# Prompt attention: all matmuls of a unit in one fixed order on TensorE

## The chip, the cores and the metric

One core of one Trainium2 chip runs the kernel as a single program on five engines: TensorE (PE), VectorE (DVE), ScalarE (ACT), GpSimd (POOL) and SyncE (SP, which mostly issues transfers). Each engine runs its own instructions in the order in which they stand in its program and waits on the others by semaphores. The metric is the device time of one launch in microseconds (us); lower is better.

## What is computed

One layer of a hybrid decoder, for a prompt of 2048 tokens and a small decode batch. The change touches the prompt attention: 8 heads of 64, three dilated window patterns, and a merge of the three outputs by their softmax denominators. Cut to that:

```python
PATTERNS = ((128, 1), (512, 4), (2048, 16))
def dilated_prompt(q, k, v, window, dil):      # blocks of n = window // dil = 128 queries
    ...
    s = jnp.einsum('brhcie,brhcje->brhcij', qb, kk) * (E ** -0.5)   # keys: block before and own block
    ...
    s = jnp.where(mask, s, NEG)
    lse = jax.nn.logsumexp(s, axis=-1)
    p = jnp.exp(s - lse[..., None])
    o = jnp.einsum('brhcij,brhcje->brhcie', p, vv)
    ...
def combine_patterns(results):
    outs = jnp.stack([o for o, _ in results], axis=0)
    lses = jnp.stack([l for _, l in results], axis=0)
    w = jax.nn.softmax(lses, axis=0)
    return jnp.sum(w[..., None] * outs, axis=0)
```

After the attention come the output projection `w_o`, norms and a gated feed-forward network.

## The kernel before

**Stages.** The trace shows dense projections and sweeps up to about 780 us, the prompt attention from there to about 1140 us, and then the output projection and the feed-forward network, in which TensorE is nearly always busy, to the end. The change touches the middle stage alone.

**Units.** Heads are taken in four pairs `pr` 0 to 3. A pair goes through three patterns (`pat` 0 to 2) of four groups `g`. A group has two units in patterns 0 and 1, and one in pattern 2: 20 units per pair, 80 in all. They are numbered u0 to u79 here, so pair 0 ends with u19, pair 1 with u39, pair 2 with u59. `qk_` of a unit makes, for each of two heads, the scores in a PSUM tile `pas` (8 matmuls of up to 256 columns per unit in patterns 0 and 1, 16 of 128 in pattern 2; three buffers), the row minima of the masked, negated scores on DVE (into `ass`, six buffers) and the exponentials on ACT, in place. `t` turns these with 8 transposes per unit into `pat` (PSUM) and copies them to `apt` on ACT or DVE. `pv` multiplies by the values into `pao` (8 matmuls, each of which the trace shows as two records); at a group's end DVE copies `pao` to the output tile `aop` of the pattern.

**Shared buffers.** Outputs of the patterns rotate through five `aop` buffers, so that the copy for pattern 2 of pair 2 waits until the merge of pair 1 has last read pattern 1 of pair 1 (line 1215), pattern 0 of pair 2 until the merge of pair 0 has last read its output (line 1217), and pattern 0 of pair 3 until the merge of pair 1 has. In patterns 1 and 2 the queries come from gathered copies `aqg` that POOL makes (line 1118, two per group, five buffers, emitted two groups ahead): a gather waits until the scores of 2.5 groups earlier are done.

**The merge.** When a pair is done, `at_merge` runs beside the next pair's units: eight small matmuls (lines 1127, 1130), small steps on DVE and POOL (lines 1136 to 1166), weights written to memory (line 1184, POOL's queue) and read back broadcast (line 1173, POOL's queue), then on POOL twelve multiplies (line 1211), four adds (line 1215), four adds into `amo` (line 1217) and four stores (line 1219). `amo` has one buffer, which the merge's first steps share: each line 1217 waits until the store before it has landed, and a merge can't begin before the last store of the merge before has landed. They are called M0 to M3 here. M3 differs: it makes its weights on POOL and ACT (lines 1206, 1204), spreads them on TensorE (line 1208), multiplies on DVE (line 1209), and its last two adds into `amo` are on DVE (line 1217). The output projection's first part reads back what M3 stored.

**What sets the order.** The units are emitted in a software pipeline: `skew=(2, 2)` means that the transposes of the unit two back are emitted behind a unit's scores, followed by the values of that unit. The emitted order binds no engine: a scheduler works out, before the run, a fixed order for each engine from an estimate of when operands come, and tile buffers and data dependences are its only limits. So on TensorE scores, transposes and values of several units are mixed.

## Time and profile before

| | us |
|---|---|
| three runs | 2859.22, 2867.0, 2854.1 |
| median | 2859.22 |
| profiled execution, its own time | 2860.6 |
| span of its trace | 2858.6 |
| granted TensorE clock, mean | 0.978 of full |

The profiled execution's time is 2.0 us longer than the span of the trace, and 1.4 us above the median of the three runs. Over the whole span TensorE is busy 2726.4 us (95%), DVE 1854.4 (65%), ACT 1279.2 (45%) and POOL 598.6 (21%). These shares say little of the attention, which is about an eighth of the span: it must be read stretch by stretch. Line numbers below and in the text are those of the kernel before.

### The profile page before, as it was taken

The numbers are of one execution on the slowest core, as the hardware profiler recorded it, in microseconds if no ns is written. First come the engines' busy times: TensorE is split into PE (matmuls) and PEld (weight loads), VectorE is DVE, ScalarE is ACT, GpSimd is POOL, SyncE is SP. The second block draws the span as 40 slices with busy tenths as digits, with TensorE's granted clock in tenths as the row PEclk, the third lists the DMA queues.
The fourth block names the chain that finished last, engine by engine and source line by source line (L and its number), as shares of the span: only waits on it lengthen the run. The fifth ranks groups of instructions, "written<-read, shape, count | busy, mean of one in ns | idle before, by whom it ended". The sixth has DMA issues, their size and how long they took to land. (4 is left out here: it accounts for less than half of the span.)

```text
span 2858.6 us, 58660 instructions
## 1 busy us (share of the span) xinstructions
PE 2726.4 (95%) x22255; PEld 2545.2 (89%) x22255; DVE 1854.4 (65%) x4557; ACT 1279.2 (45%) x2958; POOL 598.6 (21%) x751
## 2 busy tenths in 40 slices
PE   7999999999998988899899999999999999999997
PEld 6788899787877766899799999999999999999997
DVE  7657654443355656456899888776667766666666
ACT  6535433332266765344565544443344433443332
POOL 3424242443324466112210003000020000200001
PEclk9999999999999998999899999999999999999998
DMA  8755445898888655347588758787587875876654
GB/s 296 252 179 188 163 147 168 309 335 321 281 176 177 145 128 111 99 154 268 188 309 300 248 208 308 276 294 266 194 321 282 294 261 192 325 256 218 217 193 146
DMA packets 285657, 657.09 MB, mean 230 GB/s; under 512 B 31856, under 2 KB 82672, under 8 KB 283328
## 3 DMA queue, kind: packets, MB, share of 16 engines
q1 hardware_dynamic: 254880, 576.50, 59.9%
q0 software_dynamic: 13408, 44.99, 5.2%
q10 hardware_dynamic: 17088, 31.86, 3.0%
q8 instruction: 175, 2.87, 0.4%
q14 instruction: 106, 0.87, 0.1%
HBM read 509.29 MB, written 143.94 MB: 229 GB/s over the span
## 5 line engine op out<-in xcount | busy, mean ns | idle before, releaser
L68 ACT ACTIVATE ws<-wr 128x512 fp32r<-128x512 f32 (+1 forms) x482 | 293.4, 616 | 437.0 <-PE pfe L1559 132.5
L90 PE MATMUL pfd<-hh,ws 128*128 128x264 f32 x2816 | 476.2, 285 | 9.2 <-ACT ws L68 5.4
L90 PEld LDWEIGHTS pfd<-hh,ws 128*128 128x128 f32 x2816 | 400.3, 189 | 12.6 <-ACT ws L68 7.0
L71 DVE TENSOR_TENSOR ws<-wr,ws 128x512 fp32r<-128x512 f32 (+1 forms) x482 | 319.7, 669 | 137.4 <-ACT ws L68 134.5
L90 PE MATMUL pfd<-hl,ws 128*128 128x264 f32 x1408 | 303.8, 285 | 0.8 <-DVE hl L71 0.8
L1559 PE MATMUL pfa<-xh,ws 128*128 128x264 f32 x1496 | 292.9, 287 | 6.7 <-ACT ws L68 3.4
L1559 PE MATMUL pfe<-xh,ws 128*128 128x264 f32 x1496 | 289.3, 286 | 0.3 <-DVE u L1546 0.3
L1559 PE MATMUL pfd<-xh,ws 128*128 128x264 f32 x1408 | 288.4, 285 | 0.7 <-DVE up L1546 0.5
L1559 PEld LDWEIGHTS pfa<-xh,ws 128*128 128x128 f32 x1496 | 237.3, 190 | 8.6 <-ACT ws L68 5.1
L1559 PEld LDWEIGHTS pfe<-xh,ws 128*128 128x128 f32 x1496 | 237.1, 190 | 0.6 <-DVE u L1546 0.6
L396 PE MATMUL pv<-wh,xh 128*128 128x256 f32 (+1 forms) x816 | 234.0, 287 | 1.1 <-DVE th L693 1.1
L1559 PEld LDWEIGHTS pfd<-xh,ws 128*128 128x128 f32 x1408 | 231.2, 189 | 1.4 <-DVE up L1546 0.7
L396 PE MATMUL pv<-wl,xh 128*128 128x256 f32 (+1 forms) x816 | 231.5, 284 | 0.0
L396 PE MATMUL pv<-wh,xl 128*128 128x256 f32 (+1 forms) x816 | 230.8, 283 | 0.0
L90 PEld LDWEIGHTS pfd<-hl,ws 128*128 128x128 f32 x1408 | 226.1, 189 | 1.1 <-DVE hl L71 1.0
L1786 ACT ACTIVATE ass<-ass,aml 128x256 f32<-128x256 f32 (+1 forms) x384 | 174.2, 456 | 112.5 <-DVE aml L1781 85.1
L1508 POOL DMA_DIRECT2D xl<-d_xst x52 | 28.6, 551 | 889.1 <-PE pfe L1559 854.9
L1559 PE MATMUL pfd<-xl,ws 128*128 128x264 f32 x704 | 200.6, 285 | 0.0
L1781 DVE CUSTOM_DVE_ANT_0 ass<-pas,atab 128x256 f32<-128x256 f32 (+1 forms) x384 | 128.5, 363 | 90.9 <-PE pas L1780 81.0
L90 PE MATMUL pq<-xh,wh 128*128 128x512 f32 (+2 forms) x480 | 174.4, 370 | 10.1 <-ACT xh L234 7.8
L1559 PE MATMUL pfa<-xl,ws 128*128 128x264 f32 x616 | 176.6, 287 | 0.5 <-DMA xl<-d_xst 0.5
L1559 PE MATMUL pfe<-xl,ws 128*128 128x264 f32 x616 | 175.6, 285 | 0.0
(335 smaller groups left out, 6767.8 us busy)
## 6 DMA issues: line engine op xcount, KB each, us to landing
ws<-d_wst SPq DMA_DIRECT2D x248, 512.0 KB
wr<-in_wu SPq DMA_DIRECT2D x114, 512.0 KB
d_wst<-ws SPq DMA_DIRECT2D x88, 512.0 KB
wr<-in_wd SPq DMA_DIRECT2D x160, 256.0 KB
wr<-in_wt SPq DMA_DIRECT2D x60, 512.0 KB
wh<-d_wbs SPq DMA_DIRECT2D x35, 512.0 KB
wl<-d_wbs SPq DMA_DIRECT2D x35, 512.0 KB
skp<-in_ckt SPq DMA_DIRECT2D x16, 1024.0 KB
```

The source lines that it names most:

```text
L68: h = nc.scalar.activation(hi, src, AF.Copy)
L71: return h, (nc.gpsimd if lo_eng == "p" else nc.vector).tensor_tensor(lo, src, hi.bitcast(F32), op=ALU.subtract)
L90: mm = nc.tensor.matmul(o, ww[:, k, :], xx[:, s0:s0 + n], start=(k == order[0] and i == 0), stop=(k == order[-1] and i == 2))
L396: mm = nc.tensor.matmul(ps[:m, :256], x[:, t0:t0 + m], w[:, k % 4, :], start=(k == 0 and i == 0), stop=(k == KT - 1 and i == 2))
L1508: self.nc.gpsimd.dma_start(t.bitcast(F32), xo[i, z])
L1559: self.lastmm = nc.tensor.matmul(bank[:, :H], w[:, ww, k, :], xx, start=new and k == 0 and j == 0, stop=k == 3 and j == 2, skip_group_chec ...
L1781: red = nc.vector.tensor_tensor_reduce(ssb[:, sc:sc + nk], ps[:, sc:sc + nk], L.amk[self.pat][:, 256 - nk:256], scale=1.0, scalar=3e38, op ...
L1786: ex = nc.scalar.activation(ssb[:, sc:sc + nk], ssb[:, sc:sc + nk], AF.Exp, bias=self.ml[:, idx, h:h + 1], scale=-1.0, accum_out=self.ml[: ...
```

## The change

A new method `line` ties every score matmul, transpose and value matmul of the units to the one emitted before it, without a semaphore, so that the scheduler must keep them on TensorE in the order of emission: the scores of both heads of unit n, the transposes of unit n-2, the values of unit n-3. The small matmuls of the merges and those of the output projection are not tied. `qk_` emits the scores of both heads first, then minima and exponentials; `ass` is allocated with them. The skew becomes (2, 3), and `drain` calls for the transposes once ahead of its loop.

```diff
-    AB = dict(..., skew=(2, 2), ...)
+    AB = dict(..., skew=(2, 3), ...)
...
             def drain(n):
                 nonlocal pend
+                if len(fifo) > sk[0]:
+                    fifo[-1 - sk[0]].t()
                 while len(fifo) > n:
-                    if len(fifo) > sk[0]:
-                        fifo[-1 - sk[0]].t()
                     un = fifo.pop(0)
...
+    def line(self, mm):
+
+        if self.L.atpe is not None:
+            self.L.after(mm, self.L.atpe)
+        self.L.atpe = mm
...
+        scores = []
         for h in range(2):
             ps = pp.tile([128, 512], F32, name=L.n("pas"), tag="as", bufs=AB["ps"])
-            ssb = p1.tile([128, 512], F32, name=L.n("ass"), tag="ass", bufs=AB["s"])
             info = []
+            scores.append((ps, info))
             for bb in range(nbk):
...
                 for z in range(2):
-                    nc.tensor.matmul(ps[:, sc:sc + nk], lq, rk[z], start=(z == 0), stop=(z == 1))
+                    self.line(nc.tensor.matmul(ps[:, sc:sc + nk], lq, rk[z], start=(z == 0), stop=(z == 1)))
+                info.append((self.u * nbk + bb, idx, sc, nk, keys))
+        for h, (ps, info) in enumerate(scores):
+            ssb = p1.tile([128, 512], F32, name=L.n("ass"), tag="ass", bufs=AB["s"])
+            for blk, idx, sc, nk, keys in info:
                 red = nc.vector.tensor_tensor_reduce(
...
-                    nc.tensor.transpose(ptp[:, len(tl), :], ...)
+                    self.line(nc.tensor.transpose(ptp[:, len(tl), :], ...))
...
-                nc.tensor.matmul(po[64 * h:64 * h + 64, blk, :], ...)
+                self.line(nc.tensor.matmul(po[64 * h:64 * h + 64, blk, :], ...))
```

The number of instructions stays the same on TensorE, DVE, POOL and SP. What moves is the order. Names in the rows below: `pas` scores, `pat` transposes, `pao` values, `ass` exponentials, `aqg` gathered queries, the number behind a name is its tile. Lines 1780, 1803 and 1820 of before are 1787, 1813 and 1830 of after.

TensorE in pattern 2 of the last pair, before (units 77 and 78):

```order
L1803 MATMUL pat_2408_13677<-c_ident_85,ass_2388_13534 128x128
L1780 MATMUL pas_2387_13533<-akh_2069_12040,aqg_2350_13356 128x128
L1780 MATMUL pas_2387_13533<-akl_2090_12134,aqg_2350_13356 128x128
L1803 MATMUL pat_2411_13694<-c_ident_85,ass_2394_13575 128x128
L1780 MATMUL pas_2393_13574<-akh_1999_11717,aqg_2371_13447 128x128
L1780 MATMUL pas_2393_13574<-akl_2022_11825,aqg_2371_13447 128x128
```

The same engine there after, the end of one unit's scores, the transposes of the unit two back and the first values of the unit three back:

```order
L1787 MATMUL pas_2394_13574<-akh_2068_12024,aqg_2372_13440 128x128
L1787 MATMUL pas_2394_13574<-akl_2090_12125,aqg_2372_13440 128x128
L1813 MATMUL pat_2397_13601<-c_ident_85,ass_2375_13460 128x128 x4
L1813 MATMUL pat_2399_13608<-c_ident_85,ass_2376_13469 128x128 x4
L1830 MATMUL pao_2392_13558<-apt_2389_13549,av_2298_13133 64x128
L1830 MATMUL pao_2392_13558<-apt_2391_13556,av_2298_13133 64x128
```

Before, single transposes stand between the scores of single blocks, of two units at once; after, 16 scores, 8 transposes and 8 values follow one another. Over the attention, TensorE goes from another kind of matmul to values 145 times before and about once per unit, 80 times, after.

POOL at M1, before, from the small steps to the reading of the weights:

```order
L1162 TENSOR_TENSOR amm_1972_11591<-amm_1972_11591,adn_1974_11599 128x32
L1118 COPY aqg_2050_11945<-aqs_1817_10828 128x512
L1166 TENSOR_TENSOR aaw_1973_11594<-aaw_1973_11594,amm_1972_11591 128x32 x3
L1118 COPY aqg_2071_12048<-aqs_1750_10512 128x512
L1184 DMA d_awd_73<-awt_1976_11611 96x128
L1173 DMA awb_1977_11614<-d_awd_73 64x12x128 x2
```

The same place after:

```order
L1162 TENSOR_TENSOR amm_1991_11672<-amm_1991_11672,adn_1993_11680 128x32
L1166 TENSOR_TENSOR aaw_1992_11675<-aaw_1992_11675,amm_1991_11672 128x32 x3
L1118 COPY aqg_2071_12034<-aqs_1815_10809 128x512
L1118 COPY aqg_2092_12133<-aqs_1740_10458 128x512
L1184 DMA d_awd_73<-awt_1995_11692 96x128
L1118 COPY aqg_2093_12135<-aqs_1815_10809 128x512
L1118 COPY aqg_2112_12224<-aqs_1740_10458 128x512
L1173 DMA awb_1996_11695<-d_awd_73 64x12x128 x2
```

Two more gathers (`aqg_2048`, `aqg_2070`) stand in front of this, between lines 1155 and 1160. So six gathers stand ahead of M1's first line 1173 after, and two before; the last of the six, by its buffer, waits for the scores of u53. Four gathers fewer follow behind it, within M1.

POOL at the end of M2, before:

```order
L1219 DMA d_mixa_77<-amo_2225_12813 128x512
L1215 TENSOR_TENSOR aop_1949_11479<-aop_1949_11479,aop_2047_11937 128x4x128 x2
L1217 TENSOR_TENSOR amo_2247_12918<-aop_1949_11479,aop_2132_12320 128x4x128
L1206 TENSOR_SCALAR awb_2427_13778<-aaw_2425_13763 128x512
L1206 TENSOR_SCALAR awb_2432_13804<-aaw_2425_13763 128x512
...
L1219 DMA d_mixa_77<-amo_2247_12918 128x512
```

The same place after:

```order
L1219 DMA d_mixa_77<-amo_2245_12899 128x512
L1215 TENSOR_TENSOR aop_1948_11469<-aop_1948_11469,aop_2045_11918 128x4x128 x2
L1217 TENSOR_TENSOR amo_2267_13004<-aop_1948_11469,aop_2132_12311 128x4x128
L1219 DMA d_mixa_77<-amo_2267_13004 128x512
L1217 TENSOR_TENSOR amo_2297_13126<-aop_1948_11469,aop_2132_12311 128x4x128
L1219 DMA d_mixa_77<-amo_2297_13126 128x512
L1206 TENSOR_SCALAR awb_2427_13778<-aaw_2425_13763 128x512
```

M2's second and third stores now stand ahead of M3's line 1206, where the second stood behind four of them. On DVE, the copies of pattern 2 of pair 3 to `aop` stood behind all of M3's small steps; now two of the four stand right behind its line 1151 and one behind line 1155.

## Rows read from the trace of the kernel before

**Rows 1.** Busy time by stretch: window, its length, then busy us and number of instructions for PE, PE's weight loads, DVE, ACT and POOL, the granted TensorE clock, the DMA engines' busy share and GB/s.

```profile
820.00:900.00 80.00, 79.92 (x722) 66.66 (x721) 56.02 (x246) 60.75 (x229) 23.51 (x32) 1.00 0.77 165
900.00:920.00 20.00, 11.43 (x89) 8.70 (x89) 7.07 (x25) 7.38 (x26) 13.51 (x13) 0.79 0.75 165
1020.00:1060.00 40.00, 31.41 (x258) 24.87 (x256) 21.77 (x96) 24.55 (x96) 28.41 (x27) 0.98 0.66 160
...
1140.00:1180.00 40.00, 28.08 (x207) 25.91 (x204) 27.48 (x36) 14.49 (x22) 8.57 (x9) 0.83 0.43 146
```

**Rows 2.** Timeline of PE at the places where it starts again after idle time: start, busy us, line, operation, and in brackets the idle time before and what ended it.

```profile
807.40 0.77 PE L1780 MATMUL pas<-akl,aqs 128*128 128x256 f32 x2 [1.30 <-DMA akl<-d_kl]
917.73 0.47 PE L1780 MATMUL pas<-akh,aqg 128*128 128x128 f32 x1 [8.57 <-POOL aqg L1118]
1061.19 0.58 PE L1780 MATMUL pas<-akh,aqs 128*128 128x256 f32 x1 [6.90 <-DVE aml L1781]
1138.11 1.12 PE L1820 MATMUL pao<-apt,av 128*64 128x128 f32 x8 [5.74 <-DVE aop L63]
1164.75 0.59 PE L1405 MATMUL pbo<-xl,wh 128*128 128x264 f32 x1 [9.95 <-DVE xl L71]
```

**Rows 3.** The score matmuls alone (line 1780) in four stretches: window, length, busy us and number of score matmuls, the same of their weight loads, granted clock, DMA share, GB/s. The first two windows are pair 0 from u4 on, patterns 0 and 1 and then mostly pattern 2, up to the end of u19's scores; the third runs from the end of u47's scores to that of u55's (pattern 1 of pair 2); the fourth holds pattern 2 of pair 3, up to the end of u79's.

```profile
807.40:847.50 40.10, 19.12 (x98) 14.74 (x98) 0.93 0.80 169
847.50:863.70 16.20, 9.36 (x63) 8.13 (x62) 1.00 0.51 118
983.20:1009.40 26.20, 12.31 (x65) 8.93 (x65) 1.00 0.64 135
1097.00:1129.50 32.50, 15.07 (x65) 11.95 (x64) 0.80 0.42 94
```

**Rows 4.** Timeline of PE in pair 0 at full clock: a run of values and the next transposes, two scores, a run of four transposes and the next score. The difference of two starts is what a row takes of PE.

```profile
838.20 1.09 PE L1820 MATMUL pao<-apt,av 128*64 128x128 f32 x14
839.22 0.33 PE L1803 MATMUL pat<-c_ident,ass 128*128 128x128 f32 x1
...
842.90 0.28 PE L1780 MATMUL pas<-akh,aqg 128*128 128x256 f32 x1
843.02 0.28 PE L1780 MATMUL pas<-akl,aqg 128*128 128x256 f32 x1
...
846.72 0.66 PE L1803 MATMUL pat<-c_ident,ass 128*128 128x128 f32 x4
847.13 0.31 PE L1780 MATMUL pas<-akh,aqg 128*128 128x128 f32 x1
```

**Rows 5.** Groups of instructions by line and shape from 780 to 1165 us: busy us, mean ns of one, then idle time before them and what ended it. The gathers on POOL, and the exponentials of pattern 2's blocks on ACT.

```profile
L1118 POOL CAST aqg<-aqs 128x512 fp32r<-128x512 f32 x64 | 68.8, 1094 | 74.2 <-PE pas L1780 46.2 <-DMA aqs<-d_ql 13.5 <-DMA aqs<-d_qh 6.9
...
L1786 ACT ACTIVATE ass<-ass,aml 128x128 f32<-128x128 f32 x168 | 66.3, 396 | 61.8 <-DVE aml L1781 35.3 <-DMA akh<-d_kh 25.6
```

**Rows 6.** Timeline of POOL in M0: its first multiplies, four of the gathers between them, and the last add into `amo`.

```profile
904.59 3.73 POOL L1211 TENSOR_TENSOR aop<-aop,awb 128x512 f32<-128x512 f32 x3 [10.62 <-DMA awb<-d_awd]
940.75 1.06 POOL L1118 CAST aqg<-aqs 128x512 fp32r<-128x512 f32 x1 [1.75 <-PE pas L1780]
...
952.75 1.11 POOL L1118 CAST aqg<-aqs 128x512 fp32r<-128x512 f32 x1 [1.85 <-PE pas L1780]
955.15 1.13 POOL L1118 CAST aqg<-aqs 128x512 fp32r<-128x512 f32 x1 [1.29 <-PE pas L1780]
958.04 1.14 POOL L1118 CAST aqg<-aqs 128x512 fp32r<-128x512 f32 x1 [1.76 <-PE pas L1780]
...
970.21 1.29 POOL L1217 TENSOR_TENSOR amo<-aop,aop 128x512 f32<-128x512 f32 x1 [8.91 <-DMA d_mixa<-amo]
```

**Rows 7.** Timeline of POOL in M1: first small step, the weights' write and reads, first multiplies, the last two stores.

```profile
984.99 0.25 POOL L1155 TENSOR_TENSOR aaw<-aw,amm 128x32 f32<-128x32 f32 x1 [12.64 <-DVE amm L1152]
...
993.43 0.56 POOL L1184 DMA_DIRECT2D d_awd<-awt  x1 [1.51 <-DVE awt L63]
996.49 2.99 POOL L1173 DMA_DIRECT2D awb<-d_awd  x4 [2.50 <-DMA d_awd<-awt]
...
1006.51 3.77 POOL L1211 TENSOR_TENSOR aop<-aop,awb 128x512 f32<-128x512 f32 x3 [4.84 <-DMA awb<-d_awd]
...
1054.06 0.56 POOL L1219 DMA_DIRECT2D d_mixa<-amo  x1 [0.30 <-POOL amo L1217]
...
1060.37 0.56 POOL L1219 DMA_DIRECT2D d_mixa<-amo  x1 [0.30 <-POOL amo L1217]
```

**Rows 8.** Timeline of POOL at the end of M2 and in M3: M2's first store, M3's first weights, M2's second store, M3's first add into `amo`.

```profile
1123.03 0.61 POOL L1219 DMA_DIRECT2D d_mixa<-amo  x1
...
1137.05 2.38 POOL L1206 TENSOR_SCALAR awb<-aaw 128x512 f32<-128x512 f32 x4 [9.65 <-DVE aaw L1166]
1139.37 0.60 POOL L1219 DMA_DIRECT2D d_mixa<-amo  x1
...
1150.71 1.31 POOL L1217 TENSOR_TENSOR amo<-aop,aop 128x512 f32<-128x512 f32 x1 [1.88 <-DMA d_mixa<-amo]
```

**Rows 9.** Timeline of DVE: the copy of pattern 0 of pair 3 to `aop`, M3's first step, M3's last add into `amo`.

```profile
1060.10 0.69 DVE L63 COPY aop<-pao 128x512 f32<-128x512 f32 x1 [8.41 <-POOL amo L1217]
1132.48 0.42 DVE L1136 TENSOR_TENSOR atm<-pam,atab 128x256 f32<-128x256 f32 x1 [0.98 <-PE pam L1130]
1163.06 1.10 DVE L1217 TENSOR_TENSOR amo<-aop,aop 128x512 f32<-128x512 f32 x1 [2.53 <-DMA d_mixa<-amo]
```

More of the change, by code (lines that the diff above doesn't have):

```diff
@@ L954, in gla_sample @@
         yield
-    AB = dict(mw=1, qg=5, vsb=5, mq='p', klh=1, q=2, v=6, s=6, pt=5, op=5, ps=3, ppt=2, po=2, am=1, skew=(2, 2), man=(), ea=3, ed=5, mp=12, aa=(1, 4, 7, 9, 10), ms='ppps', mv=2, em=1)
+    AB = dict(mw=1, qg=5, vsb=5, mq='p', klh=1, q=2, v=6, s=6, pt=5, op=5, ps=3, ppt=2, po=2, am=1, skew=(2, 3), man=(), ea=3, ed=5, mp=12, aa=(1, 4, 7, 9, 10), ms='ppps', mv=2, em=1)
     def px(self, name, dt=F32):
@@ L1259, in ssq_add @@
             return (nc.gpsimd if eng == "p" else nc.vector).tensor_tensor(ssq[:, :w], ssq[:, :w], sq[:, :w], op=ALU.add)
-    pnmm = pbmm = None
+    pnmm = pbmm = atpe = None
     lastmm, gk = None, "g"
@@ L1783, in qk_ @@
                     scale=1.0, scalar=3e38, op0=ALU.add, op1=ALU.min, accum_out=self.ml[:, idx, h:h + 1])
-                info.append((self.u * nbk + bb, idx, sc, nk, keys))
             for blk, idx, sc, nk, keys in info:
@@ L1802, in t @@
                 for j, kb in enumerate(keys):
-                    nc.tensor.transpose(ptp[:, len(tl), :], ssb[:, sc + 128 * j:sc + 128 * j + 128], L.ident)
+                    self.line(nc.tensor.transpose(ptp[:, len(tl), :], ssb[:, sc + 128 * j:sc + 128 * j + 128], L.ident))
                     tl.append((blk, kb, j == 0, j == len(keys) - 1))
@@ L1819, in pv @@
                 blk, kb, st, sp = tl[j]
-                nc.tensor.matmul(po[64 * h:64 * h + 64, blk, :], L.vq[self.base + kb][:, 64 * h:64 * h + 64], pt[:, j, :],
-                                 start=st, stop=sp)
+                self.line(nc.tensor.matmul(po[64 * h:64 * h + 64, blk, :], L.vq[self.base + kb][:, 64 * h:64 * h + 64],
+                                           pt[:, j, :], start=st, stop=sp))
         if self.u < self.nu - 1:
```

## Prediction, made before the changed kernel ran

> **What bounds the kernel now.** I read the busy time by stretch first. In [rows 1] PE is busy for 79.92 of 80 us from 820 to 900, but only 11.43 of 20 from 900 to 920, 31.41 of 40 from 1020 to 1060 and 28.08 of 40 from 1140 to 1180. So the attention is limited by PE in pair 0 and in the middle of each pair, and by something else in three places. The timeline of PE names it [rows 2]: an 8.57 us wait at 917.73 for a gather on POOL, 6.90 at 1061.19 for row minima on DVE, 5.74 at 1138.11 for a copy to `aop`, and 9.95 at 1164.75 for DVE's part of the output projection. Each leads to the merges. The 8.57 us are a gather queued on POOL behind M0's first multiplies [rows 6]. At 1061.19 DVE itself had stood 8.41 us for POOL's last line 1217 of M1 [rows 9], since `aop` was not free. At 1164.75 DVE had waited for the store ahead of its last line 1217 [rows 9]. The reader is to see a serial chain: M0, M1 and M2 share one `amo`, so each begins when the last store of the one before has landed, and M3's stores end the stage. The dense part behind 1164.75 is almost untouched by the change and moves rigidly with it. So I sum what the chain of merges gains or loses, not what PE does.
>
> **The change part by part.**
>
> *Order on PE.* No matmul is removed. From [rows 4]: a score takes 0.12 us (842.90 to 843.02), four transposes 0.41 (846.72 to 847.13), 14 value records 1.02, the step out of the run included. A full unit of patterns 0 and 1 then costs 8 x 0.12 + 2 x 0.41 + 16/14 x 1.02 = 2.95 us, and about 0.1 to enter the values: 3.0. Half of pattern 1's units have one-key blocks (6 transposes, 12 value records) and cost 2.5, so pattern 1 averages 2.8. A pattern 2 unit has 16 scores of a little under 0.12: 3.8 on PE, and on ACT 8 exponentials of 0.396 [rows 5] and a share of the copies: about 3.7. Steps between values and other work cost about 0.2 us per run; 145 runs become 80, which is 65 x 0.2 = 13 us over the stage, already inside these paces.
>
> *Start of M0.* PE takes up u4 at 807.40, when a key transfer lands [rows 2]; the change doesn't touch that transfer. Before, the score counts of [rows 3] give 98/8 = 12.2 units in 40.1 us (3.3 each), then 63/16 = 3.9 in 16.2 us (4.1 each). After: 4 x 3.0 + 8 x 2.8 + 4 x 3.8 = 49.6 us against 56.3 up to the end of u19. The chain starts **7 us earlier** (0 if PE keeps its present pace, 10 if the gaps of pattern 2 vanish too).
>
> *M0.* Its POOL work is the same. Between its multiplies stand gathers that wait for PE's scores: 1.75 + 1.85 + 1.29 + 1.76 = 6.65 us in four rows [rows 6]. With PE up to date in that stretch these mostly go; I take **-6** (0 to -7). The 8.57 us wait of PE stays, and grows: the gather still lies behind M0's first multiplies, which move 7 us, while PE arrives some 12 earlier (u20 to u31, twelve units at 2.9 instead of 3.3, on top of the 7). That costs nothing, as M1 waits for M0's end and not for PE.
>
> *M1.* Here the change costs. Six gathers now stand ahead of its first line 1173, two before; POOL is in order, so the writing (line 1184) and reading of the weights are queued behind them, and M1's multiplies behind those. The sixth waits for u53's scores. PE can't be far ahead: the copies of pattern 0 of pair 2 stand on DVE until M0's last line 1217, about 9 us ahead of M1's first step (970.21 ends M0's adds, M1's first small step on POOL is at 984.99 [rows 6, 7]). From that release about ten units must pass; at 2.75 us that is 27, against 996.49 - 971.5 = 25 before, plus a gather of 1.09 [rows 5] and the issue: **+4**. At the pace of [rows 3], third window (65/8 = 8.1 units in 26.2 us, 3.2 each), it is +9. Four gathers fewer then lie inside M1's multiplies: 4 x 1.09 = **-4**. Net 0 (-4 to +7).
>
> *M2.* One gather instead of two ahead of its reads, one more behind: **-1** (-3 to +2).
>
> *End of M2 and M3.* M2's second store came 16.3 us after its first (1123.03 to 1139.37), 9.65 of which POOL stood at line 1206 for M3's weights [rows 8]. Now the second and third stores stand ahead of line 1206; where nothing intervenes a store follows the last in 6.3 us (1054.06 to 1060.37 [rows 7]). That could give 16.3 - 6.3 = 10. What is late next is M3 itself: two copies to `aop` now stand behind its line 1151 on DVE and wait for M2's last line 1215, and the last transposes and values are tied behind each other. These were after M3's small steps before. I give back half: **-5** (0 to -10).
>
> *The rest.* Minima behind both heads' scores start 4 x 0.12 = 0.5 us later per unit. Two units now lie between scores and transposes and hide that; without this cover it would be 80 x 0.5 = 40 us. Later values hold one more pair of `apt`, of which there are five; a unit takes two, and the transposes of the next unit wait for none. The earlier `drain` call moves no work by itself.
>
> Sum: -7 - 6 + 0 - 1 - 5 = -19. The profiled execution took 2860.6 (span 2858.6 and 2.0 around it), 1.4 above the median: 2841.6, so **2842**.
>
> *A rule weighed.* At 917.73 PE idles 8.57 us at one score [rows 2], and nothing else runs on it in that time. The Trainium skill ("TensorE: Matmul & The Clock Gate", "Step-by-step: what each phase is for") says that matmuls stay in program order and only weight loads are pulled ahead. By that rule a fixed line speaks against itself: at each stall a whole unit of transposes and values, some 2 us, is held back and runs late. At the two stalls that end on the chain (1061.19 and 1138.11) that would be +4, a sum of -15. The trace agrees that nothing passed the waiting score, but I keep -19, since work held back there runs beside M2 and M3.
>
> **The rivals.**
>
> *The chain shrinks with PE.* Gathers on POOL waited 46.2 us for PE in all [rows 5]. If the merges are long only because of that, all of it goes: 2860.6 - 46 = 2815. For it: pattern 2 of pair 3 runs at 65/16 = 4.1 units in 32.5 us, 8 each [rows 3], where 3.8 would do. Against: 8.91 us waits for landed stores and 10.62 for weights [rows 6] are not PE's. Chance 0.12.
>
> *Nothing arrives.* PE runs ahead, and the time turns into longer waits for gathers and `aop` at u32, u61 and u64, because M0 to M2 keep their length and M3's copies eat the end. Only the start's 7 us and little else remain: 2850 to 2862. For it: three of the five restarts in [rows 2] end on POOL's work. Chance 0.25.
>
> *Slower: M1 waits for PE, and PE for DVE.* The six gathers make M1's weights wait for u53, and any unit in between that waits for DVE (its in-order copies behind `aop`, M1's small steps between minima) adds in full. With p us per unit the term is 10 x (p - 2.75) beside the +4: the whole gain is gone at p = 2.75 + 1.9 = 4.65, and at the 8 us of pattern 2 in pair 3 [rows 3] the time is 2842 + 52 = 2894. These are pattern 0 and 1 units with a present pace of 3.2, so I give 0.13 to a p of over 4.65, with 2868 at 5.4.
>
> *The change doesn't do what it says.* Were the old order already this one, all would stay at 2860. The order shows otherwise on PE and on POOL: 0.02, in with "nothing arrives".
>
> **How the numbers follow.** Forecast (2830 to 2850) 0.50, chain shrinks 0.12, nothing arrives 0.25, slower 0.13. Of the range, low 2815 is the second case, high 2868 is M1 at +7, the start at 0, M0 at 0, and a slower pace of 5.4 in the rival. About 0.5% (14.3 us) is what a measurement of this kernel can tell from no change, so faster is below 2845: the second case and most of the first, 0.12 + 0.43 = 0.55. Same, up to 2873.5, takes the rest of the first, all of the third and a part of the slower: 0.35. Slower 0.10.
>
> **What would show it.** Right: M0's first multiplies 7 us earlier than 904.59; gathers in M0 with little wait for PE; M1's first line 1173 about 29 us behind M0's last line 1217 instead of 25; M2's second store some 7 us behind its first; PE taking up the output projection at about 1146. Runs of values near 80, with pattern 2 at 3.8 us per unit wherever no copy to `aop` is waited for. Wrong: M1 longer than 90 us; line 1206 still ahead in time of M2's second store; M3's small steps standing behind copies for 10 us; or dense PE behind the restart that takes longer than before, which would put the cause outside the attention.

## The result, and the profile after

The changed kernel takes **2841.6 us** (median of six runs, 2835.1 to 2849.3) against 2861.9 for the kernel before in six runs beside them (2854.1 to 2867.0). The ratio is 0.9929, with a 95% interval of 0.9912 to 0.9945, so it is faster by 0.7%, more than the half per cent set as the limit. The forecast was 2842, in a range of 2815 to 2868. The profiled execution of after took 2844.3, span 2842.5: 16.1 less span than the profiled execution of before. For one experiment (e8) the profiled execution was disturbed (5246.2 us), so it is left out of the median and its trace is not used.

Line numbers of after are shifted: scores are line 1787 (1780 before), minima 1792 (1781), exponentials 1796 (1786), transposes 1813 (1803), values 1830 (1820). The merges keep theirs (1118, 1155, 1173, 1184, 1206, 1211, 1217, 1219).

Busy time by stretch, with the columns of [rows 1]:

```profile
820.00:900.00 80.00, 76.01 (x786) 67.56 (x784) 59.62 (x273) 66.14 (x259) 26.31 (x35) 0.99 0.82 166
900.00:920.00 20.00, 13.25 (x114) 11.57 (x114) 7.23 (x32) 8.20 (x30) 18.62 (x19) 0.71 0.91 178
1020.00:1060.00 40.00, 21.45 (x203) 18.66 (x203) 18.60 (x68) 14.65 (x51) 18.42 (x26) 0.73 0.35 94
1140.00:1180.00 40.00, 37.31 (x290) 37.31 (x291) 17.72 (x21) 17.44 (x30) 0.00 (x0) 0.91 0.30 97
```

From 900 to 920 it is busy 13.25 us instead of 11.43, and 1140 to 1180 is now nearly all dense work (37.31 instead of 28.08). But it is no longer full from 820 to 900 (76.01 instead of 79.92, for 786 matmuls instead of 722), and 1020 to 1060 has fallen from 31.41 to 21.45 us. PE gets through its units sooner and then stands. Where it stands is in the timeline of PE, in the order of [rows 2]:

```profile
805.57 0.55 PE L1787 MATMUL pas<-akl,aqs 128*128 128x256 f32 x1 [1.75 <-DMA akl<-d_kl]
...
906.75 0.47 PE L1787 MATMUL pas<-akh,aqg 128*128 128x128 f32 x1 [10.75 <-POOL aqg L1118]
...
1036.91 0.48 PE L1830 MATMUL pao<-apt,av 128*64 128x128 f32 x2 [22.78 <-DVE aop L63]
...
1142.69 0.59 PE L1405 MATMUL pbo<-xl,wh 128*128 128x264 f32 x1 [7.63 <-DVE xl L71]
```

The wait for the gather, 8.57 us, is now 10.75. The 22.78 us at 1036.91 are the values of pair 2 that wait for the copies of its pattern 2 to `aop`, which wait for M1 to free the buffers (line 1215). Before, PE came to the same place as the buffers came free:

```profile
1044.90 2.06 PE L1820 MATMUL pao<-apt,av 128*64 128x128 f32 x32 [0.49 <-DVE aop L63]
```

The waits of 6.90 and 5.74 us of [rows 2] are gone. Both waits that are left were longer, and the end still came earlier: PE comes out of its last wait in the output projection at 1142.69 instead of 1164.75, **22.1 us sooner**. So these 33 us of idle PE lie beside the merges and not on the path. What set the time is read from POOL, in the same places as [rows 6, 7]:

```profile
897.10 4.92 POOL L1211 TENSOR_TENSOR aop<-aop,awb 128x512 f32<-128x512 f32 x4 [9.84 <-DMA awb<-d_awd]
...
952.73 1.29 POOL L1217 TENSOR_TENSOR amo<-aop,aop 128x512 f32<-128x512 f32 x1 [6.24 <-DMA d_mixa<-amo]
...
966.17 0.24 POOL L1155 TENSOR_TENSOR aaw<-aw,amm 128x32 f32<-128x32 f32 x1 [11.30 <-DVE amm L1152]
...
968.74 2.25 POOL L1118 CAST aqg<-aqs 128x512 fp32r<-128x512 f32 x2 [1.90 <-PE pas L1787]
...
974.60 2.17 POOL L1118 CAST aqg<-aqs 128x512 fp32r<-128x512 f32 x2 [0.52 <-PE pas L1787]
978.64 0.56 POOL L1184 DMA_DIRECT2D d_awd<-awt  x1 [1.87 <-DVE aml L1792]
980.36 2.11 POOL L1118 CAST aqg<-aqs 128x512 fp32r<-128x512 f32 x2 [1.16 <-PE pas L1787]
983.18 1.52 POOL L1173 DMA_DIRECT2D awb<-d_awd  x2 [0.70 <-DMA d_awd<-awt]
...
1022.10 3.70 POOL L1211 TENSOR_TENSOR aop<-aop,awb 128x512 f32<-128x512 f32 x3 [4.87 <-DMA awb<-d_awd]
1028.99 3.70 POOL L1211 TENSOR_TENSOR aop<-aop,awb 128x512 f32<-128x512 f32 x3 [3.19 <-DMA awb<-d_awd]
...
1046.83 0.56 POOL L1219 DMA_DIRECT2D d_mixa<-amo  x1 [0.30 <-POOL amo L1217]
```

M0's first multiplies start at 897.10 (904.59 before). M0's last add into `amo` starts at 952.73 (970.21); no gather with a wait for PE stands between M0's multiplies any more. In M1 the gathers at 968.74, 974.60 and 980.36 now lie between the first small step (966.17) and the reads of the weights (983.18), as the forecast said. Behind the reads stand two waits for landed weights that were not foreseen, 4.87 us at 1022.10 and 3.19 at 1028.99.

The end of M2 and M3, on POOL and then on DVE, as in [rows 8] and [rows 9]:

```profile
1110.66 0.61 POOL L1219 DMA_DIRECT2D d_mixa<-amo  x1
1111.29 2.48 POOL L1215 TENSOR_TENSOR aop<-aop,aop 128x512 f32<-128x512 f32 x2
...
1116.18 0.57 POOL L1219 DMA_DIRECT2D d_mixa<-amo  x1 [0.30 <-POOL amo L1217]
...
1120.61 0.56 POOL L1219 DMA_DIRECT2D d_mixa<-amo  x1 [0.30 <-DVE aaw L1166]
1121.19 2.38 POOL L1206 TENSOR_SCALAR awb<-aaw 128x512 f32<-128x512 f32 x4
...
1129.87 1.80 POOL L1217 TENSOR_TENSOR amo<-aop,aop 128x512 f32<-128x512 f32 x1 [1.89 <-DMA d_mixa<-amo]
```

```profile
1109.40 0.42 DVE L1136 TENSOR_TENSOR atm<-pam,atab 128x256 f32<-128x256 f32 x1 [2.48 <-PE pam L1130]
...
1111.29 2.55 DVE L1151 TENSOR_TENSOR amm<-aw,aml 128x32 f32<-128x32 f32 x1
1113.81 1.05 DVE L63 COPY aop<-pao 128x512 f32<-128x512 f32 x1
...
1119.50 1.05 DVE L1166 TENSOR_TENSOR aaw<-aaw,amm 128x32 f32<-128x32 f32 x3
...
1141.00 1.10 DVE L1217 TENSOR_TENSOR amo<-aop,aop 128x512 f32<-128x512 f32 x1 [2.53 <-DMA d_mixa<-amo]
```

M2's second store follows its first after 5.5 us (1110.66 to 1116.18) instead of 16.3, and line 1206, which stood ahead of it in time, comes at 1121.19, behind the third store. Copies to `aop`, from 1113.81 on, stand among M3's small steps on DVE behind line 1151, as expected. The steps were held, but for less than 10 us: from line 1136 to the end of line 1166 they take 11.1 us (1109.40 to 1120.55), where before they took 4.6 (1132.48 [rows 9] to 1137.07). Of the 6.6 more, 2.4 are line 1151, which took 2.55 us instead of 0.18, just while POOL did its two adds of line 1215. M3's last add is at 1141.00 instead of 1163.06.

### The profile page after: what moved, and what is told of

The parts are those of the page before. It is cut to its first block, busy times and chain, and to the rows that moved or that the text cites. A ratio compares the mean times of both kernels' runs of the same rounds, so it can differ in the third digit from the quotient of the medians.

```text
span 2842.5 us, 58662 instructions
## 1 busy us (share of the span) xinstructions
PE 2682.9 (94%) x22255; PEld 2529.1 (89%) x22255; DVE 1841.9 (65%) x4557; ACT 1268.1 (45%) x2958; POOL 602.3 (21%) x751
## 5 line engine op out<-in xcount | busy, mean ns | idle before, releaser
L90 PE MATMUL pq<-xl,wh 128*128 128x512 f32 (+2 forms) x480 | 173.7, 363 | 0.0
```

What stands on the lines that cost most here:

```text
L90: mm = nc.tensor.matmul(o, ww[:, k, :], xx[:, s0:s0 + n], start=(k == order[0] and i == 0), stop=(k == order[-1] and i == 2))
```

## The experiments

All times are medians; ratios are to the kernel before on the same chip, with the 95% interval. "Restart" is the time at which PE comes out of its last wait in the first part of the output projection (line 1405, which waits there for `xl`) in the trace (e3 and e8 aren't read for it): 1164.75 before, 1142.69 after. It leaves out what follows the attention, which no variant edits and which took between 1691.3 us (e11) and 1705.0 (e5) in the twelve traces that show both. But it is one trace each: e7, whose time agrees with that of the changed kernel, has a restart 5.9 us earlier, so differences of that size show nothing by themselves. The last column is the granted TensorE clock of whole runs, averaged over the runs of the row; over 60 runs of the kernel before it is 0.9756.

| run | median | ratio | restart | mean clock |
|---|---|---|---|---|
| changed kernel | 2841.6 | 0.9929 (0.9912 to 0.9945) | 1142.7 | 0.9735 |
| e1, later values on before | 2874.6 | 1.0034 (1.0017 to 1.0051) | 1173.2 | 0.9722 |
| e2, scores first on before | 2853.4 | 0.9972 (0.9957 to 0.9987) | 1156.5 | 0.9765 |
| e3, fixed order on before | 3083.9 | 1.0774 (1.0752 to 1.0796) | - | 0.9487 |
| e4, after without the fixed order | 2850.9 | 0.9958 (0.9941 to 0.9974) | 1151.5 | 0.9773 |
| e5, after without M0 to M2's multiplies | 2828.2 | 0.9880 (0.9848 to 0.9912) | 1132.2 | 0.9740 |
| e6, before without M0 to M2's multiplies | 2835.3 | 0.9906 (0.9878 to 0.9935) | 1133.8 | 0.9820 |
| e7, after with 5 value buffers | 2845.7 | 0.9944 (0.9923 to 0.9965) | 1136.8 | 0.9739 |
| e8, e7 and two `amo` | 2824.3 | 0.9878 (0.9847 to 0.9910) | - | 0.9760 |
| e9, after, gathers behind M1's reads | 2837.9 | 0.9922 (0.9896 to 0.9947) | 1136.3 | 0.9748 |
| e10, e8 and e9 together | 2835.7 | 0.9902 (0.9880 to 0.9925) | 1127.9 | 0.9745 |
| e11, before, two `amo`, 5 value buffers | 2863.5 | 0.9997 (0.9983 to 1.0010) | 1159.2 | 0.9740 |
| e12, e8 with stores on SP's queue | 2824.7 | 0.9858 (0.9838 to 0.9878) | 1124.1 | 0.9775 |

**One part alone, on the kernel before.** e1 takes only the later values, e2 only the scores of both heads ahead of the minima, e3 only the fixed order.

```diff
# e1
-skew=(2, 2)
+skew=(2, 3)
+                if len(fifo) > sk[0]:
+                    fifo[-1 - sk[0]].t()
                 while len(fifo) > n:
-                    if len(fifo) > sk[0]:
-                        fifo[-1 - sk[0]].t()
# e2
+        scores = []
         for h in range(2):
...
+            scores.append((ps, info))
...
+        for h, (ps, info) in enumerate(scores):
...
+            for blk, idx, sc, nk, keys in info:
                 red = nc.vector.tensor_tensor_reduce(
# e3, and the same at the transposes and the values
-                    nc.tensor.matmul(ps[:, sc:sc + nk], lq, rk[z], ...)
+                    self.line(nc.tensor.matmul(ps[:, sc:sc + nk], lq, rk[z], ...))
...
```

Expected of e1:

> The kernel before with the skew of (2, 3) and the earlier call for transposes alone; matmuls untied, minima as before. Theory (the chain of merges sets the time, by its start, by what stands on POOL ahead of its steps, and by its end): the start of M0 stays near 904.6 us for its first multiplies, two gathers stand ahead of M1's reads as before, but M2's second store now stands ahead of M3's line 1206, so the end gains 5 to 10 us: 2850 to 2857. Rival (TensorE's order itself is what pays: 146 runs of values are still 151 here): no change, 2858 to 2865.

Expected of e2:

> The kernel before with both heads' scores emitted first and the minima behind them; skew (2, 2), matmuls untied. Theory of the chain: eight gathers stand ahead of M1's reads (two before, six in the changed kernel), which adds 4 to 10 us to M1, and M3's weights stand between M2's stores, so nothing comes back at the end: 2858 to 2872. Rival (TensorE's order pays): 150 runs of values, but 448 changes between kinds of matmuls instead of 619, each at 0 to 0.1 us: 2845 to 2860.

Expected of e3:

> The kernel before with its matmuls tied in the order of emission and nothing else; skew (2, 2), minima as before. TensorE then has 86 runs of values, nearly as few as the changed kernel's 80. Theory of the chain: the order on POOL is what matters, and there all gathers of a pair now stand behind the last store of the merge before it, so TensorE stands through most of each merge, and the next merge starts later by as much: over 2900, about 2950. Rival (TensorE's order pays): as fast as the changed kernel or nearly, 2838 to 2850.

None of the three gives the result. e1 came out slower, at 2874.6, against both theories (some 5 of its 10 us go with its lower clock, an estimate by the slope in the last section): M0's first multiplies stay at 904.4, the later values make M0's last store 6 us later (977.8), and though the second store of M2 follows the first in 4.7 us, the third comes 17.0 us behind it, and the restart is at 1173.2. e2 gives 0.3%: M0's first multiplies come at 893.7, 10.9 us earlier than before, but M1's reads at 1002.0 are 5.5 later, so only 8.2 is left at the restart (1156.5). The theory that the chain would eat it all (2858 to 2872) missed; the rival's 2845 to 2860 holds. e3 is 7.7% slower. That it would be over 2900 was foreseen (about 2950), the reason not. The waits of PE by what they wait for (total us, times, longest; scores are line 1786 here, minima 1787):

```profile
PE pas L1786 <- DVE aml L1787: 126.4, 224, 1.6
```

Tied in the old order, each head's scores stand behind the minima that free a `pas` buffer, and PE waits for that 224 times, 0.6 us each on average: 126 of some 220 us lost. The fixed order by itself is harmful; with the minima behind both heads' scores and the later values together it gains. Which of the two it needs wasn't run.

**The change without the fixed order.**

```diff
-                    self.line(nc.tensor.matmul(ps[:, sc:sc + nk], lq, rk[z], ...))
+                    nc.tensor.matmul(ps[:, sc:sc + nk], lq, rk[z], ...)
```

and the same at the transposes and the values.

Expected of e4:

> The changed kernel without the ties: skew (2, 3), scores first, minima behind; 145 runs of values. Theory of the chain: six gathers ahead of M1's reads as in the changed kernel, M0 starting at most 3 us earlier than before, M3's weights between M2's stores: 2852 to 2866. Rival (the emission, not the ties, makes the gain): 2840 to 2846, the time of the changed kernel.

2850.9 lies between the two expectations. POOL's timeline of e4 at the end of M2:

```profile
1109.25 0.61 POOL L1219 DMA_DIRECT2D d_mixa<-amo  x1
...
1121.28 1.22 POOL L1206 TENSOR_SCALAR awb<-aaw 128x512 f32<-128x512 f32 x2 [4.49 <-DVE aaw L1166]
...
1126.07 0.61 POOL L1219 DMA_DIRECT2D d_mixa<-amo  x1
```

M2's first store is at 1109.25, 1.4 us earlier than in after. So up to there the two other parts, together, give all that the change gives. Then line 1206 stands ahead of the second store again, waits 4.49 us for M3's weights, and the store comes 16.8 us after the first. The fixed order is worth 8.8 us of restart (1151.5 to 1142.7), all of it, in this pair of traces, behind the first store, where line 1206 now stands behind the other stores on POOL. By time alone the two are hardly apart: the ends of their intervals overlap (0.9941 to 0.9974, 0.9912 to 0.9945).

**How much the merges weigh.** e5 and e6 leave out POOL's 12 multiplies by the weights (line 1211) in each of M0 to M2, so the outputs of those pairs are unweighted.

```diff
-                    (nc.gpsimd if j % 12 < AB["mp"] else nc.vector).tensor_tensor(
-                        OP[i][:, :, sl], OP[i][:, :, sl], W[:, i], op=ALU.mult)
+                    pass
```

Expected of e5:

> The changed kernel without the twelve multiplies on POOL of M0, M1 and M2 (line 1211 of before), so that the three patterns are merged without their weights for pairs 0 to 2; the weights are still made, written and read. Theory (the merges' chain sets the time): each of three merges loses 12 x 1.22 = 14.7 us and more, until TensorE binds: 76 units from u4 at 2.95, 2.8 and 3.8 us end 233 us behind 807, M3 takes some 37 more, and the output projection starts near 1080 instead of 1142.7, so 2842 - 62 = 2780. Rival (TensorE sets the time already and the merges run beside it): within 10 us of 2842.

Expected of e6:

> The kernel before without the same multiplies. Theory: units at the old pace, 60 at 3.3 and 16 at 4.1 us or more, end about 264 us behind 807, and the output projection starts near 1110 instead of 1164.75: 2805. The difference to the changed kernel without multiplies, some 25 us, is what the order on TensorE is worth when no merge binds. Rival (the merges run beside TensorE): within 10 us of 2861, and the difference stays at 20.

Both missed: each lies between the theory's time and the rival's. The 36 multiplies are 44.6 us of POOL in after; without them after gains 13 us and before 26, and the two orders are 7 us apart, 1.6 at the restart (1132.2 and 1133.8). So the merges' work on POOL is a limit in both orders, but another stands close behind it. The two are also not at one clock (0.974 and 0.982 over whole runs; 0.87 and 0.96 from 780 to 1140 in their traces, where after and before with the multiplies show 0.90 and 0.93). In e5's trace PE waits 5.52 us for a transfer of values at 918.92, and then, in the windows of PE alone (window, length, busy us and number, granted clock, DMA share, GB/s):

```profile
910.00:920.00 10.00, 4.43 (x43) 0.93 0.61 146
920.00:925.00 5.00, 5.00 (x28) 0.50 0.53 164
...
940.00:945.00 5.00, 5.00 (x32) 0.50 0.31 75
...
950.00:955.00 5.00, 5.00 (x54) 1.00 0.60 159
```

PE is busy for every microsecond at half clock for 25 us, from 920 to 945. In the kernel before, the windows from 920 to 925 and from 925 to 930 show 0.81 and 1.00. The traced run is the slowest of e5's four (2839.1, the others 2826.8 to 2828.9), so the median may have less of this.

**Which wait of the chain.** Two `amo` buffers let a merge write while the last store still lands. They take the room of one value buffer, so e7 is the control.

```diff
# e7
-v=6
+v=5
# e8: e7, and at the four places of the tag
-tag="amo", bufs=1
+tag="amo", bufs=2
# e9
-            self.nc.gpsimd.tensor_copy(t, src)
+            c = self.nc.gpsimd.tensor_copy(t, src)
+            if self.wrd is not None and (pat, g, h) == (1, 2, 1):
+                self.after(c, self.wrd)
+                self.wrd = None
...
-                    nc.gpsimd.dma_start(W[64 * h:64 * h + 64],
+                    d = nc.gpsimd.dma_start(W[64 * h:64 * h + 64],
...
+                    if pr == 1 and not cb:
+                        self.wrd = d
```

Expected of e7:

> The changed kernel with five buffers for the values instead of six, as the control of the next run (the room for a second amo comes from it); the order of instructions on POOL is the same. Every theory: within 5 us of 2842. It is also a second trace of the changed order: if the 5 us that the trace of the changed kernel gave back around 1470 us were chance in POOL's small steps (L107 to L110), they are not here; if they come from the earlier start, they are.

Expected of e8:

> The changed kernel with five buffers for the values and two for amo. Theory of the chain: an add into amo no longer waits for the store right ahead of it (21.7 us of such waits on POOL and 7.0 on DVE in the changed kernel), and a merge no longer waits for the landing of the last store of the one before: some 5 to 8 us less for each of M1, M2 and the end: 2815 to 2830. Rival (TensorE or the copies to aop bind just as late): 2838 to 2845.

Expected of e9:

> The changed kernel with one tie more: the gather of the second head of pattern 1, group 2 of pair 2 stands behind M1's first two reads of its weights, so that the six gathers no longer stand ahead of them. Theory: the reads come 4 us earlier against M1's first small step (17.0 us in the changed kernel: 966.17 to 983.18), M1 ends about 4 us earlier, and the time falls by 2 to 5 us: 2837 to 2840. Rival (the gathers cost nothing there, as TensorE is the later of the two, or TensorE loses at u53 what M1 gains): 2841 to 2846.

The control agrees with after. e8 gives 2824.3, inside what the theory of the store waits expected (2815 to 2830): it is 21 us below the control, and the two intervals don't touch. e9 sits within its expected 2837 to 2840, but its interval overlaps that of e7 and of after, so its time settles nothing. Its trace does. POOL in e9 (lines 1158, 1189 and 1176 are after's 1155, 1184 and 1173):

```profile
965.32 0.25 POOL L1158 TENSOR_TENSOR aaw<-aw,amm 128x32 f32<-128x32 f32 x1 [11.38 <-DVE amm L1155]
...
974.22 0.56 POOL L1189 DMA_DIRECT2D d_awd<-awt  x1 [3.18 <-DVE awt L63]
979.55 3.00 POOL L1176 DMA_DIRECT2D awb<-d_awd  x4 [4.77 <-DMA d_awd<-awt]
```

From the first small step of M1 to the weights' write (line 1184) it takes 8.9 us, where after takes 12.5 (966.17 to 978.64) and before 8.4 [rows 7]. So the gathers ahead of the write cost 3.6 us, as far as one pair of traces tells.

**Both, and the old order.** e10 puts e8 and e9 together. e11 puts e8's edit on the kernel before. e12 issues e8's stores from SP.

```diff
# e12: e8, and
-ms='ppps'
+ms='ssss'
```

Expected of e10:

> The changed kernel with two buffers for amo and five for the values (as in e8), and the tie of e9 that keeps the gathers behind M1's first two reads. Theory of the chain: the gains of e8 (some 19 us under its control) and of e9 (3 to 5) add, since one shortens the ends of the merges and the other the start of M1: 2820 to 2826. Rival (once the stores are off the chain, TensorE's own wait for the late gathers binds): 2826 to 2835, not below e8.

Expected of e11:

> The kernel before, with its untied order, with two buffers for amo and five for the values. Theory: the waits for landed stores are on the chain in either order, so it gains as the changed kernel did, some 15 to 20 us: 2841 to 2848. Rival (the store waits bind only in the tied order, where the gathers' waits are gone; in the old order gathers and units take up the time): 2853 to 2862.

Expected of e12:

> e8 with all stores of the merges issued by SyncE instead of POOL (pairs 0 to 2; pair 3's are there already). Theory: POOL saves twelve issues of 0.58 us, seven us on the chain, and the stores no longer stand between its multiplies: 2816 to 2824. Rival (SyncE's queue holds key and value loads that wait for buffers, so stores and with them the next adds come later): 2828 to 2850.

e10 at 2835.7 missed its 2820 to 2826 and is just above the rival's 2835; its runs lie from 2826.9 to 2847.1 and its interval overlaps e8's, so whether the moved gathers harm is open. e11 is the one that decides: the edit that gives 21 us in the new order gives nothing in the old (0.9997), where the theory wanted 2841 to 2848. The clock of whole runs is hardly the reason: 0.9740 against 0.9749 in the runs of before beside them, worth 1 to 2 us by the slope in the last section. What holds e11 at the end is seen on POOL, M2's last two stores and M3's first weights:

```profile
1121.45 1.09 POOL L1219 DMA_DIRECT2D d_mixa<-amo  x2
1144.22 2.38 POOL L1206 TENSOR_SCALAR awb<-aaw 128x512 f32<-128x512 f32 x4 [21.68 <-DVE aaw L1166]
```

The stores are out 26.8 us earlier than before (1148.23), but POOL then stands 21.68 us for M3's weights, which need the last units of pair 3, and the restart is only 5.5 us earlier (in e11's fastest run, which is the traced one). So at the end the merges no longer bind, and the units on PE do. Their pattern 2 in the last pair, first all engines (columns of [rows 1]), then the score matmuls alone (columns of [rows 3]):

```profile
1100.00:1136.00 36.00, 30.12 (x201) 23.55 (x196) 17.12 (x80) 19.58 (x78) 22.36 (x22) 0.80 0.32 79
```

```profile
1100.00:1136.00 36.00, 16.11 (x68) 12.74 (x68) 0.80 0.32 79
```

68 scores in 36 us are 4.25 units at 8.5 us, about the 8 of before [rows 3]. That is not what a unit costs PE, as the same 36 us hold 42 transposes and 91 value records, over five units' worth. An estimate: at the prediction's prices (0.12 us a score, 0.41 for four transposes, 1.02 for 14 value records) all of it takes 19 us at full clock and 24 at the granted 0.80. PE is busy for 30.1, so some 6 us are left for the mixed order, and 5.9 are short waits for minima, exponentials and copies (the longest 0.8). So clock, mixing and waits have about the same share there. Another loss lies ahead of it: from 1020 to 1045 the clock is at a mean of 0.53 with PE nearly always busy (last section). How much of e11's null result is the order alone stays open.

The same units of e12, all engines and then the scores:

```profile
1081.00:1096.00 15.00, 14.09 (x143) 12.76 (x139) 9.58 (x64) 13.79 (x62) 14.88 (x13) 1.00 0.33 99
```

```profile
1081.00:1096.00 15.00, 8.23 (x64) 7.52 (x64) 1.00 0.33 99
```

The 64 scores of four units take 15 us at full clock, 3.75 each, the 3.8 that the prediction worked out for PE alone. e12's 2824.7 is 0.7 over its expected 2816 to 2824, and its interval (0.9838 to 0.9878) lies wholly below that of the change (0.9912 to 0.9945). It has the lowest ratio, 1.4% below the kernel before, but e8 without its edit has 2824.3 and an interval that overlaps: the seven us that moving the stores to SP should have saved are not shown.

## Why the prediction was right, point by point

The terms, each measured from the end of the one ahead of it in the traces of before and after:

| term | forecast | measured | from |
|---|---|---|---|
| start of M0 | -7 | -7.5 | 904.59 to 897.10 |
| M0 | -6 | -10 | its last store, 971.79 to 954.31 |
| M1 | 0 | +3.9 | 1060.37 to 1046.83 |
| M2, to its first store | -1 | +1.2 | 1123.03 to 1110.66 |
| end of M2 and M3 | -5 | -9.7 | 1164.75 to 1142.69 |
| dense tail | 0 | +6.0 | span behind the restart, 1693.9 to 1699.8 |
| sum | -19 | -16.1 | span; the medians differ by 20.3 |

The chain was the right thing to sum, and the sum is right within what the runs tell apart, but not each term; errors of both signs cancel. That 2842 came within half a us of the median is luck: M0 and the end gave 8.7 us more than forecast, M1, M2 and the tail took 12.1 back in the traced pair.

*Start of M0* held, and so did its pace. The scores of u19 end at 855.67 in after, 50.1 us behind u4's first at 805.57, where 49.6 was worked out and before took 56.3. The score matmuls alone, up to the end of u15's and of u19's, as in [rows 3]:

```profile
805.60:841.00 35.40, 14.22 (x91) 11.70 (x91) 0.95 0.83 169
841.00:855.70 14.70, 7.97 (x65) 7.45 (x64) 1.00 0.69 152
```

Twelve units of patterns 0 and 1 in 35.4 us are 2.95 each, where the prediction has 34.4 us for the twelve, and four of pattern 2 in 14.7 are 3.7, where it has 3.8 (some score records are missing, so the units are counted by time). So u19's scores end 8.0 us earlier, 6.2 of them by pace; the other 1.8 have another source: the key transfer that u4 waits for landed 1.8 earlier (805.57 instead of 807.40 [rows 2]). e2 gets 10.9 us here from the scores alone, e1 nothing.

*M0* was mis-sized: -10 and not -6. The term was the gathers' waits, and all of them went. By line, from M0's first multiplies to its last store, before and then after (904 to 973 and 897 to 955 us):

```profile
L1118 POOL CAST aqg<-aqs 128x512 fp32r<-128x512 f32 x16 | 17.1, 1084 | 9.5 <-PE pas L1780 7.4 <-issue 2.2
L1217 POOL TENSOR_TENSOR amo<-aop,aop 128x512 f32<-128x512 f32 x4 | 5.2, 1290 | 8.9 <-DMA d_mixa<-amo 8.9
```

```profile
L1118 POOL CAST aqg<-aqs 128x512 fp32r<-128x512 f32 x16 | 16.9, 1089 | 0.0
L1217 POOL TENSOR_TENSOR amo<-aop,aop 128x512 f32<-128x512 f32 x4 | 5.2, 1292 | 9.2 <-DMA d_mixa<-amo 9.2
```

The forecast had taken four waits, 6.65 us, and of these 6; POOL had stood 9.5 us ahead of gathers, 2.2 of them with no wait that the profile names. The waits for landed stores, which the forecast had held fixed, stayed as they were in sum (8.9 and 9.2).

*M1* is where a step failed: "four gathers fewer then lie inside M1's multiplies: -4". The +4 ahead of it came as said: from M0's last store to M1's reads it is 28.9 us instead of 24.7 ("about 29 instead of 25"). But the shorter multiplies did not shorten M1 in step, since POOL then stood for the landing of the next weights, 4.87 and 3.19 us, a wait that the term had at nothing. The four reads issued ahead of them took 12.7 us (median) to land instead of 8.4; meanwhile the DMA engines moved 224 GB/s (1008.5 to 1029) instead of 139 (1019.2 to 1030), but that this slowed them is not shown. From first multiplies to last store it is 52.0 us instead of 53.9, and the wait ahead of the first multiplies is 5.85 instead of 4.84. Nor was the whole +4 the gathers': e9 puts them at 3.6 us up to the write, and with them behind the reads the way from write to reads takes 5.3 us (3.1 before; 4.5 in the changed kernel). So M1, from store to store, takes 92.5 us, over the 90 that I had set as a sign of being wrong (88.6 before); M0 and the end made up for it.

*M2* is small in both, +1.2 for -1.

*End of M2 and M3* was mis-sized in the giving back. The 10.8 us between the stores came whole (forecast 10), and of the five that I gave back for M3's copies only 1.1 was taken: 24.8 us from M2's second store to M3's last add instead of 23.7. M3's small steps did take 6.6 us longer, as feared, but most of that lay beside M2's stores. e4 shows it for the fixed order, in one pair of traces; the later values alone (e1) also bring the second store close, but not the third.

*The dense tail* did not move rigidly in this trace, the second of the signs set for being wrong; but of the twelve traces only e11's tail is shorter than before's, and those of the variants of after, which leave it as it is, differ among themselves by 8 us. One piece has a name: PE's broadcast matmul waits for two small steps on POOL, 128x5 elements each, that took 2.15 and 2.42 us, here PE and then POOL in after,

```profile
1472.55 0.69 PE L143 MATMUL pb<-c_ident,rcy 128*128 128x128 f32 x2 [3.94 <-POOL rcy L110]
```

```profile
1467.85 2.15 POOL L109 TENSOR_SCALAR rcz<-rcz 128x5 f32<-128x5 f32 x1
1470.08 2.42 POOL L110 TENSOR_TENSOR rcy<-rcz,rcy 128x5 f32<-128x5 f32 x1
```

and 0.33 and 0.52 in e7, where PE does not wait:

```profile
1459.57 0.33 POOL L109 TENSOR_SCALAR rcz<-rcz 128x5 f32<-128x5 f32 x1
1459.98 0.52 POOL L110 TENSOR_TENSOR rcy<-rcz,rcy 128x5 f32<-128x5 f32 x1
```

This wait is there in after, e1, e4, e5, e10 and e12, 3.9 to 5.2 us, and under 1 us in before, e2, e6, e7, e9 and e11. It goes with no edit, so I take it for chance. It is part of the 6.0 us of the tail in the profiled execution of after.

*The rivals.* "Nothing arrives" was right that PE would run ahead and stand (33 us at two places) and wrong that the merges keep their length: M0 became 10 us shorter. "The chain shrinks with PE" got little of its -46: M0's 9.5 us of gathers' waits went, but over the attention POOL's gathers still wait 38.5 us for PE. The slower case wanted a pace of 4.65 us per unit in pair 2; M1's +4 leaves no room for it. The rule that held work costs 4 at two stalls is not borne out: those two stalls are gone, the one at 1036.91 is 22.78 us long, and the restart was still 22.1 earlier.

*What the runs add.* Before the change there were two limits of nearly one size in the attention: the pace of the units on PE, worst in pattern 2 of the last pair, and the merges through one `amo`. In the old order a second `amo` gives nothing (e11), and leaving out 44 us of POOL gives 26 (e6). In the new order a second `amo` gives 21 us (e8 against e7). That it does so because the new order took PE's limit away is argued from e11's and e12's traces; e4 with two `amo` was not run. What stays open: what holds e5 at 13 us, of which its low clock may be a part, and why e10 is not e8's equal. As each variant is planned anew, the runs differ in more places than their edits; what rests on one row of a trace is shown, what rests on a sum of edits is only argued.

## What to carry to other kernels

When an engine's order is tightened, sum the serial chain that it feeds and not its own busy time: here PE stood 33 us at two places where it had stood 9, and the end came 22 us earlier. Where two limits are near one size, an edit that gives nothing may be worth 20 us once the other is gone, so try it again after each step. A fixed order must come with the depth that it needs: the same ties cost 7.7% in a pipeline one unit shallower, with each head's scores behind the other's minima, and gained at its end in the changed one.

## What the runs showed of the hardware

Much of the spread between runs of one kernel goes with the clock. Over 60 runs of the kernel before (2848 to 2874 us) the time falls by 1.56 us for each 0.001 of a run's mean granted clock, with a correlation of -0.83; which of the two moves the other is not shown by that. By that slope, an estimate that carries it over to other kernels, the 0.008 between e6 and e5 is worth 12 us, and at one clock the two orders without multiplies would be some 19 us apart instead of 7, near the change's own 20. Single traces show stretches of low clock: besides e5's 25 us at 0.50 with PE wholly busy, e11 has PE busy 23.45 of the 25 us from 1020 to 1045 at a mean of 0.53, after PE had been busy 14.2 of the 15 us ahead.

The same two steps of 128x5 elements on POOL took 0.33 and 0.52 us in one trace and 2.15 and 2.42 in another. On DVE, a step of 128x32 elements took 2.55 us instead of 0.18 while POOL did two adds of 128x512 beside it (1111.29).
